# Row sums and first weight sums on VectorE, and a down stage with chunk-wise splits and four PSUM tiles, in a fused transformer block

## Chip, cores and metric

One core of one Trainium2 chip runs the whole kernel in one launch. The metric is the device time of that launch in microseconds (us), the median of several runs. Engines have short names: PE is TensorE (matrix products), DVE is VectorE, ACT is ScalarE, POOL is GpSimd, SP is SyncE, whose queue issues the DMAs. In the code they are T, V, A, G and S.

## What is computed

A block of a hybrid model on one sequence of 1024 tokens, 1024 features: adaptive norm, sparse attention and a gated linear attention side by side, output projection, and then the part that the change touches, a gated MLP with 2816 hidden features:

```python
x = x + g1[:, None, :] * mix
h2 = _modulate(_rms_norm(x, norm2_g[l]), sh2, sc2)
gate, up = jnp.split(h2 @ w_gate_up[l], 2, axis=-1)
x = x + g2[:, None, :] * ((jax.nn.silu(gate) * up) @ w_down[l])
return _rms_norm(x, final_g)
```

All inputs are fp32. Every large product is made of three passes: each operand is split in a high part, rounded to the type fp32r (a cast on ACT), and a low part, the rest (a subtraction on DVE or POOL), and high·high, high·low and low·high are added up in PSUM.

## The kernel before

**Mix and second norm (L1050 on).** A loop over eight token tiles t finishes the output projection of a tile (`mix_mm`, matmuls L1009 to L1011), adds it on DVE to the residual (L1012), norms it (`norm2`: square sum on ACT, scaling on POOL L1070), and stores the residual x1 to DRAM (x1_d). `norm2_T` transposes the normed tiles on PE (L1087), applies scale and shift on ACT (L1095) into the tiles `vv`, and splits them (`bsplit`, cast L1078, low part L1079).

**Gate and up (L1170 to L1222).** The two products are made by a scheme with seven products in place of eight, each of one block of weights or a sum of blocks with one block of activations or a sum of blocks. The sums of activations, t1 to t4, are the "row sums": made in `norm2_T` for the second half of the tokens, partly on DVE (L1102, L1105, L1109), partly on POOL (L1103, and the low halves of t3 and t4 in L1079). The sums of weights, s1 to s4, are made in `Pair.sum` on POOL (L1139, L1140, L1144, L1145). There are 11 pairs n of 256 hidden features; each has a gate and an up side, each with seven products k of 12 matmuls (L1170 high·high, L1171 high·low, L1172 low·high), 1848 matmuls in all. `PRODUCTS` names the operands of product k, `BANK` the PSUM bank; k = 0 and 4 use plain weights and the plain blocks 11 and 21, which are there first. The gate side takes four single PSUM banks (pool ps, 4 buffers), the up side two tiles of two banks (pool pw, 2 buffers); together that is all of PSUM. `wop` makes a weight operand: load (512 KB a half), sum if need be, cast on ACT (L1162), low part on DVE (L1163), seven products ahead. A written-out list `order` sets the sequence of products: in pair 0 product 0 and 4 of both sides, then 1, 2, 3, 5, 6 of gate and after that of up.

**Down (L1274 on).** The hidden features are 22 chunks f of 128, in groups of 2, 4, 4, 4, 4, 4. `down_ops` prepares all chunks of a group at once, while the group before is multiplied: load of 512 KB of w_down, scaling by g2 on POOL (L1292), cast on ACT (L1282) and low part on DVE (L1283); load of the hidden values from hid_d, cast and low part likewise. `down` runs over eight token tiles; for each the group's matmuls (L1319 to L1321, 6 for each chunk, 1056 in all) fill one pw tile, and DVE adds it to the residual tile x1 (L1324), which was read back before group 0 (L1278). In the last group the final norm follows (squares L1327, scaling L1304, store L1305).

Each engine works through its instructions in order. The buffers named here: g (33 tiles of 4 KB a partition), gs (4), raw (2), whi and wlo (4 each).

## Time and profile before

| what | us |
|---|---|
| median of 3 runs | 1489.37 (1487.27 to 1489.51) |
| profiled execution | 1487.22 |
| its span in the trace | 1485.5 |
| PE busy | 1346.8 (91%) |
| DVE busy | 895.8 (60%) |
| ACT busy | 563.5 (38%) |
| POOL busy | 452.9 (30%) |

The span is the time between the first and the last instruction that the profiler recorded; the execution's own time is a little longer. Busy times are shares of the whole span, through stages with different limits: what a stage waits for is read from the waits and the timeline of that stage. In a timeline an instruction stands with its start, its duration and, in brackets, how long its engine had been idle before it and who released it. Matmuls are pipelined, so their durations overlap, and the step from start to start is what one costs.

### The profile page before, as it was taken

The page shows a single profiled execution, that of the slowest core. Times are in us where ns is not written, and L with a number is a line of the kernel's source. Part 1 is how long each engine was busy: PE and PEld are TensorE (multiplying, and loading weights), DVE is VectorE, ACT ScalarE, POOL GpSimd, SP SyncE. Part 2 cuts the span into 40 slices and gives each one's busy share as a digit, 9 for nine tenths or more (in the row PEclk, how much of TensorE's full clock was granted, in tenths as well). Part 3 has the DMA queues.
Part 4 walks back from the last instruction along what each step waited for, and adds up shares of the span by engine and source line. Part 5 has one row for each costly group of instructions (what it writes and reads, how often), then busy time and mean ns, then how long its engine had stood idle before and what let it go on. Part 6 is the DMA issues. An engine that isn't in the chain of part 4 may idle for free.

```text
span 1485.5 us, 18355 instructions
## 1 busy us (share of the span) xinstructions
PE 1346.8 (91%) x6975; PEld 1124.7 (76%) x6975; DVE 895.8 (60%) x1544; ACT 563.5 (38%) x1009; POOL 452.9 (30%) x385
## 2 busy tenths in 40 slices
PE   5899856998899999999949999999999978999997
PEld 4777755797699888788837888888888856877786
DVE  4578999969538477663566445444545457345424
ACT  3466444666373333451654333333333223111201
POOL 3550531155000000140382444444444345113101
PEclk9999968998699999999978999999999998999999
DMA  9601001011013356360311222222223366113102
GB/s 267 184 15 43 15 1 29 29 29 44 15 30 101 113 151 204 104 237 1 114 42 30 85 85 85 86 86 85 85 79 106 129 233 205 57 57 113 43 3 111
DMA packets 91358, 131.11 MB, mean 88 GB/s; under 512 B 6179, under 2 KB 65666, under 8 KB 91270
## 3 DMA queue, kind: packets, MB, share of 16 engines
q1 hardware_dynamic: 91112, 129.88, 27.2%
q8 instruction: 55, 0.90, 0.2%
q14 instruction: 33, 0.27, 0.1%
q10 hardware_dynamic: 158, 0.06, 0.0%
HBM read 107.90 MB, written 22.03 MB: 87 GB/s over the span
## 4 chain that ended last, share of the span: by engine, by line
PE 60%; DVE 20%; DMA 6%; ACT 4%; POOL 4%; issue 3%; SPq 2%; DVEq 0%; ACTq 0%; POOLq 0%
PE pw L1170 5%; PE ps L1172 5%; PE ps L1170 5%; PE ps L1171 4%; PE pw L1172 4%; PE pw L1171 4%; PE pw L1319 4%; PE pw L1320 4%; PE pw L1321 4%; DVE junk_d L588 4%; DMA raw<-in_w_mod_dram 2%; DVE h L743 2%; PE pw L1009 2%; PE pw L1011 2%; PE pw L1010 2%
## 5 line engine op out<-in xcount | busy, mean ns | idle before, releaser
L617 ACT ACTIVATE junk_a<-g,Ya 128x1024 int8<-128x1024 f32 (+2 forms) x96 | 99.8, 1039 | 93.9 <-DVE Ya L624 92.9
L1324 DVE TENSOR_TENSOR g<-g,pw 128x1024 f32<-128x1024 f32 (+1 forms) x49 | 58.3, 1195 | 117.0 <-PE pw L1321 116.9
L246 PE MATMUL ps<-whi,g 128*128 128x256 f32 x384 | 114.4, 298 | 0.0
L247 PE MATMUL ps<-whi,g 128*128 128x256 f32 x384 | 113.1, 294 | 0.0
L248 PE MATMUL ps<-wlo,g 128*128 128x256 f32 x384 | 112.9, 294 | 0.0
L1292 POOL TENSOR_TENSOR raw<-raw,g 128x1024 f32<-128x1024 f32 x22 | 59.7, 2717 | 136.0 <-DMA raw<-in_w_down_dram 129.9
L1199 POOL TENSOR_TENSOR g<-g,h 128x512 f32<-128x512 f32 x33 | 52.3, 1585 | 141.7 <-DVE h L1213 66.9
L1170 PE MATMUL ps<-g,wlo 128*128 128x512 f32 x184 | 72.7, 395 | 17.4 <-ACT wlo L1162 17.4
L237 PE MATMUL ps<-g,whi 128*128 128x512 f32 x208 | 83.8, 403 | 0.0
L239 PE MATMUL ps<-g,wlo 128*128 128x512 f32 x208 | 82.6, 397 | 0.0
L238 PE MATMUL ps<-g,whi 128*128 128x512 f32 x208 | 82.1, 395 | 0.0
L1319 PE MATMUL pw<-g,g 128*128 128x512 f32 x192 | 76.4, 398 | 5.6 <-DVE g L1324 5.5
L246 PEld LDWEIGHTS ps<-whi,g 128*128 128x128 f32 x384 | 78.0, 203 | 1.6 <-issue 1.4
L1319 PE MATMUL pw<-whi,g 128*128 128x512 f32 x160 | 65.1, 407 | 14.5 <-DVE g L1324 14.0
L247 PEld LDWEIGHTS ps<-whi,g 128*128 128x128 f32 x384 | 77.9, 203 | 0.0
L248 PEld LDWEIGHTS ps<-wlo,g 128*128 128x128 f32 x384 | 77.8, 202 | 0.2 <-issue 0.2
L1320 PE MATMUL pw<-g,g 128*128 128x512 f32 x192 | 75.9, 395 | 0.0
L1321 PE MATMUL pw<-g,g 128*128 128x512 f32 x192 | 75.7, 394 | 0.0
L1172 PE MATMUL ps<-g,wlo 128*128 128x512 f32 x184 | 72.7, 395 | 3.2 <-DVE wlo L1163 3.2
L1170 PE MATMUL pw<-g,whi 128*128 128x512 f32 x184 | 73.9, 402 | 1.7 <-DVE h L1219 1.7
L954 POOL TENSOR_TENSOR raw<-raw,g 128x1024 f32<-128x1024 f32 x4 | 9.6, 2388 | 213.1 <-DMA raw<-in_w_out_dram 213.1
L1171 PE MATMUL ps<-g,wlo 128*128 128x512 f32 x184 | 72.5, 394 | 0.0
(378 smaller groups left out, 3863.1 us busy)
## 6 DMA issues: line engine op xcount, KB each, us to landing
raw<-in_w_gate_up_dram SPq DMA_DIRECT2D x40, 512.0 KB, 3.5
raw<-in_w_mod_dram SPq DMA_DIRECT2D x32, 512.0 KB, 3.6
raw<-in_w_in_dram SPq DMA_DIRECT2D x24, 512.0 KB, 3.7
hid_d<-g SPq DMA_DIRECT2D x22, 512.0 KB, 3.0
raw<-in_w_down_dram SPq DMA_DIRECT2D x22, 512.0 KB, 3.8
gs<-hid_d SPq DMA_DIRECT2D x22, 512.0 KB, 4.7
g<-in_x_dram SPq DMA_DIRECT2D x16, 512.0 KB, 6.2
g<-in_w_mod_dram SPq DMA_DIRECT2D x16, 512.0 KB, 8.6
```

Source lines behind the costliest of these rows:

```text
L237: T.matmul(pt, lhsT=wh, rhs=rh, start=(k == 0), stop=False)
L239: T.matmul(pt, lhsT=wl, rhs=rh, start=False, stop=(k == KC - 1))
L246: T.matmul(pt, lhsT=rh, rhs=wh, start=(k == 0), stop=False)
L247: T.matmul(pt, lhsT=rl, rhs=wh, start=False, stop=False)
L248: T.matmul(pt, lhsT=rh, rhs=wl, start=False, stop=(k == KC - 1))
L617: A.activation(junk_a[:, :W], score[t], AF.Sign, bias=Y[:, j:j + 1].bitcast(F32), accum_out=acc[:, j:j + 1])
L1170: T.matmul(pt, lhsT=w[:, 0, kk, :], rhs=rh, start=(not more and kk == 0), stop=False, skip_group_check=more)
L1171: T.matmul(pt, lhsT=w[:, 0, kk, :], rhs=rl, start=False, stop=False, skip_group_check=more)
L1172: T.matmul(pt, lhsT=w[:, 1, kk, :], rhs=rh, start=False, stop=(kk == 3), skip_group_check=more)
L1319: T.matmul(po[:, cc], lhsT=ah[:, r], rhs=wh[:, cc], start=(f == 0), stop=False)
L1320: T.matmul(po[:, cc], lhsT=al[:, r], rhs=wh[:, cc], start=False, stop=False)
L1321: T.matmul(po[:, cc], lhsT=ah[:, r], rhs=wl[:, cc], start=False, stop=(f == nf - 1))
```

## The change

It has three parts. (1) All row sums and their low parts are made on DVE, by `row_sums`: for the first half of the columns of blocks qq = 0 within the loop at t = 6, for the rest ("late", 128x512 and 128x1024 at a time) behind the loop, in the sequence t1, t3, 22, t2, t4. t2 takes the place of block 22 once that is split. (2) The first operands of pair 0 (products 0 and 4) come from loads of 128 columns (`first_ops`), its full weights are loaded behind the loop, its weight sums are made on DVE, its products 0 of gate and up run ahead of the last tiles' transposes and its products 4 between them, and products 1, 2, 3, 5, 6 then alternate between gate and up. PSUM banks are taken one by one. (3) In the down stage `down_op` prepares one chunk at every second token tile of the group before; odd token tiles take two ps banks and even ones a pw tile; ACT copies group 0 out of PSUM into new tiles `acc`, and x1 is read back and added in group 2.

The diff, with removed blocks shortened:

```diff
...
+X1_AT = 2
 
 C_Q, C_K, C_V, C_QI, C_KI, C_GQ, C_GK, C_GV, C_GO, C_GL = (
     0, 512, 1024, 1536, 2048, 2120, 2376, 2632, 3144, 3656)
@@ -1096,19 +1098,16 @@
                          bias=sh2[:, k:k + 1], scale=gg2[:, k:k + 1])
         if m == 0:
             bsplit(("11", "21")[kh], qq, v, cols, V)
...
+    def row_sums(names, qq, cols):
+
+        v11, v21, v12, v22 = (vv[key][:, :, cols] for key in ((0, 0, qq), (1, 0, qq), (0, 1, qq), (1, 1, qq)))
+        for name in names:
+            dst, a, b = {"t1": (v11, v12, v11), "t3": (v12, v22, v12), "22": (v22, None, None),
+                         "t2": (v22, v22, v11), "t4": (v21, v21, v22)}[name]
+            if a is not None:
+                V.tensor_tensor(dst, a, b, ALU.subtract)
+            bsplit(name, qq, dst, cols, V)
 
 
 
@@ -1124,7 +1123,12 @@
         def load(self, tag="raw"):
             self.raw = []
             for kh in range(2):
-                r = g([P, 4, 256]) if tag == "g" else g([P, 4, 256], tag="raw", bufs=NRAW)
+                if tag == "g":
+                    r = g([P, 4, 256])
+                elif tag == "ring":
+                    r = g([P, 4, 256], tag=("whi", "wlo")[kh], bufs=NW)
+                else:
+                    r = g([P, 4, 256], tag="raw", bufs=NRAW)
                 S.dma_start(r, w_gate_up[kh * 512:(kh + 1) * 512, self.c0:self.c0 + 256]
                             .rearrange("(k p) n -> p k n", p=P))
                 self.raw.append(r)
@@ -1133,16 +1137,17 @@
             return self.raw[j][:, :, i * P:(i + 1) * P]
 
         def sum(self, name):
+            E = V if self.n == 0 else G
             if name == "s1":
                 t = gs([P, 2, 4, P])
                 self.sums["s1"], self.sums["s2"] = t[:, 0], t[:, 1]
-                G.tensor_tensor(t[:, 0], self.a(1, 0), self.a(1, 1), ALU.add)
-                G.tensor_tensor(t[:, 1], t[:, 0], self.a(0, 0), ALU.subtract)
+                E.tensor_tensor(t[:, 0], self.a(1, 0), self.a(1, 1), ALU.add)
+                E.tensor_tensor(t[:, 1], t[:, 0], self.a(0, 0), ALU.subtract)
             elif name == "s3":
                 t = gs([P, 2, 4, P])
                 self.sums["s3"], self.sums["s4"] = t[:, 0], t[:, 1]
-                G.tensor_tensor(t[:, 0], self.a(0, 0), self.a(1, 0), ALU.subtract)
-                G.tensor_tensor(t[:, 1], self.a(0, 1), self.sums["s2"], ALU.subtract)
+                E.tensor_tensor(t[:, 0], self.a(0, 0), self.a(1, 0), ALU.subtract)
+                E.tensor_tensor(t[:, 1], self.a(0, 1), self.sums["s2"], ALU.subtract)
 
     uid_w = [0]
 
@@ -1181,13 +1186,15 @@
 
         def __init__(self, n, up, sg):
             self.pair, self.up, self.sg = Pair((DFF if up else 0) + n * 256, n), up, sg
-
-        def banks(self):
-            if self.up:
-                p, q = pw(), pw()
-                self.bank = [p[:, C0], p[:, C1], q[:, C0], q[:, C1]]
-            else:
-                self.bank = [ps() for _ in range(4)]
+            self.bank = [None] * 4
+
+        def banks(self, i):
+            if self.bank[i] is None and self.up:
+                p = pw()
+                self.bank[i // 2 * 2:i // 2 * 2 + 2] = [p[:, C0], p[:, C1]]
+            elif self.bank[i] is None:
+                self.bank[i] = ps()
+            return self.bank[i]
 
         def put(self, i, m, src):
             dst = self.sg[i][:, (C0, C1)[m]]
@@ -1199,10 +1206,8 @@
                 G.tensor_tensor(dst, dst, src, ALU.mult)
 
         def run(self, k, w):
-            if k == 0:
-                self.banks()
+            product(self.banks(BANK[k]), w, k)
             a, b, c, d = self.bank
-            product(self.bank[BANK[k]], w, k)
             if k == 0:
                 self.u2 = half()
                 A.copy(self.u2, a)
@@ -1227,8 +1232,7 @@
         two = [Side(n, False, None), Side(n, True, None)]
         sides.append(two)
         if n == 0:
-            order += [(s, k) for k in (0, 4) for s in two]
-            order += [(s, k) for s in two for k in (1, 2, 3, 5, 6)]
+            order += [(s, k) for k in (1, 2, 3, 5, 6) for s in two]
         elif n == NF - 1:
             order += [(s, k) for k in range(7) for s in two]
         else:
@@ -1240,22 +1244,50 @@
             s, k = todo.pop(0)
             ready.append(wop(s.pair, k, tag))
 
+    def first_ops(s):
+
+        raw = g([P, 8, P], tag="raw", bufs=NRAW)
+        S.dma_start(raw, w_gate_up[:, s.pair.c0:s.pair.c0 + P].rearrange("(k p) n -> p k n", p=P))
+        for j in range(2):
+            w = g([P, 2, 4, P], F32R)
+            A.copy(w[:, 0], raw[:, 4 * j:4 * j + 4, :])
+            V.tensor_tensor(w[:, 1], raw[:, 4 * j:4 * j + 4, :], w[:, 0].bitcast(F32), ALU.subtract)
+            first[s, 4 * j] = w
+
     xns = {}
+    first = {}
     nxt = att_pre(0)
     for t in range(NT):
         cur, nxt = nxt, att_pre(t + 1) if t + 1 < NT else None
         mix_mm(t, 0, *cur)
         xns[t] = norm2(t)
         if t == W0_AT:
...
+            for x in sides[0]:
+                first_ops(x)
         if t >= 2:
             for q in range(2):
                 norm2_T(t // 2 - 1, (2 * (t % 2) + q) if t < 6 else (q * 2 + t % 2))
-    for q in (0, 2, 1, 3):
+        if t == 6:
+            row_sums(("t1", "t3", "22", "t2", "t4"), 0, slice(0, 256))
+    sides[0][0].pair.load()
+    sides[0][1].pair.load("ring")
+    sg = [g([P, L]) for _ in range(2)]
+    for x in sides[0]:
+        x.sg = sg
+        x.run(0, first[x, 0])
+    for q in range(2):
         norm2_T(3, q)
+    late = ((0, slice(256, 512)), (1, slice(0, 512)))
+    for qq, cols in late:
+        row_sums(("t1",), qq, cols)
+    for n, x in enumerate(sides[0]):
+        x.run(4, first[x, 4])
+        norm2_T(3, 2 + n)
+    for name in ("t3", "22", "t2", "t4"):
+        for _ in range(2):
+            prepare()
+        for qq, cols in late:
+            row_sums((name,), qq, cols)
     for s, k in order:
         if k == 0 and not s.up:
             sg = [g([P, L]) for _ in range(2)]
@@ -1272,10 +1304,7 @@
 
 
     g2b = mod_bcast(1, 5 * D)
-    x1 = {}
-    for t in range(NT):
-        x1[t] = g([P, D])
-        S.dma_start(x1[t], x1_d[t * P:(t + 1) * P, :])
+    fin, acc = {}, {}
 
     def split_tile(raw, tags):
         hi, lo = (g([P, D], F32R) if tag == "g" else g([P, D], F32R, tag=tag, bufs=NW) for tag in tags)
@@ -1283,67 +1312,75 @@
         V.tensor_tensor(lo, raw, hi.bitcast(F32), ALU.subtract)
         return hi, lo
 
...
+    def down_op(n, f):
+
+        raw = g([P, D], tag="raw", bufs=NRAW)
+        S.dma_start(raw, w_down[f * P:(f + 1) * P, :])
+        G.tensor_tensor(raw, raw, g2b, ALU.mult)
+        rawh = gs([P, L])
+        S.dma_start(rawh, hid_d[f * P:(f + 1) * P, :])
+        hid = split_tile(rawh, ("g", "g"))
+        return hid, split_tile(raw, ("whi", "wlo") if n % 2 else ("g", "g"))
 
...
+    groups = [range(0, 2)] + [range(f, f + 4) for f in range(2, DFF // P, 4)]
+    NDG = len(groups)
+    cur, nxt = [down_op(0, f) for f in groups[0]], []
+    left = []
+    for n in range(NDG):
+        ending = n == NDG - 1
+        ahead = list(groups[n + 1]) if not ending else []
         for t in range(NT):
-            po = pw()
+            if t % 2 == 0 and ahead:
+                nxt.append(down_op(n + 1, ahead.pop(0)))
+            if n == X1_AT:
+                xr = gs([P, D])
+                S.dma_start(xr, x1_d[t * P:(t + 1) * P, :])
+            if t % 2:
+                po = [ps(), ps()]
+            else:
+                pq = pw()
+                po = [pq[:, C0], pq[:, C1]]
             r = slice(t * P, (t + 1) * P)
...
+            for m in range(2):
+                for f, ((ah, al), (wh, wl)) in enumerate(cur):
+                    cc = (C0, C1)[m]
+                    T.matmul(po[m], lhsT=ah[:, r], rhs=wh[:, cc], start=(f == 0), stop=False)
+                    T.matmul(po[m], lhsT=al[:, r], rhs=wh[:, cc], start=False, stop=False)
+                    T.matmul(po[m], lhsT=ah[:, r], rhs=wl[:, cc], start=False, stop=(f == len(cur) - 1))
+            if n == 0:
+                acc[t] = g([P, D])
+                for m, cc in enumerate((C0, C1)):
+                    A.copy(acc[t][:, cc], po[m])
+                continue
+            parts = [(C0, po[0]), (C1, po[1])] if t % 2 else [(slice(0, D), pq)]
+            ssq = small(2, tag="s2") if ending else None
+            for m, (cc, src) in enumerate(parts):
+                add = V.tensor_tensor(acc[t][:, cc], acc[t][:, cc], src, ALU.add)
+                if ending:
                     jk = gs([P, D], BF16)
-                    A.activation(jk[:, :w], x1[t][:, cc], AF.Square, accum_out=ssq[:, n:n + 1])
-            if last:
-                if w < D:
+                    A.activation(jk[:, cc], acc[t][:, cc], AF.Square, accum_out=ssq[:, m:m + 1])
+            if n == X1_AT:
+                V.tensor_tensor(acc[t], acc[t], xr, ALU.add)
+            if ending:
+                if len(parts) > 1:
                     V.tensor_tensor(ssq[:, 0:1], ssq[:, 0:1], ssq[:, 1:2], ALU.add)
                 left.append((t, rstd_of(ssq, D, 1)))
                 if len(left) > 1:
                     with tc.issue_after(add.ins):
                         finish_rows(*left.pop(0), D)
-        while left:
-            with tc.issue_after(add.ins):
-                finish_rows(*left.pop(0), 512 if len(left) == 0 else D)
-
-    groups = [range(0, 2)] + [range(f, f + 4) for f in range(2, DFF // P, 4)]
-    nxt = down_ops(0, groups[0])
-    for n in range(len(groups)):
-        cur, nxt = nxt, down_ops(n + 1, groups[n + 1]) if n + 1 < len(groups) else None
-        if nxt is None:
+        cur, nxt = nxt, []
+        if n == NDG - 2:
             fin["g"] = gs([P, D])
             S.dma_start(fin["g"], final_g[None, :].to_broadcast([P, D]))
-        down(*cur, nxt is None)
+    while left:
+        with tc.issue_after(add.ins):
+            finish_rows(*left.pop(0), 512 if len(left) == 0 else D)
 
 
 # ---- launch: one core; inputs and outputs as the reference has them ----
```

The order of PE where the mix ends and gate and up begins; ps_... and pw_... are PSUM tiles, L1087 (L1089 in the change) are transposes, L1170 to L1172 (L1175 to L1177) the product matmuls. Before:

```order
L1087 MATMUL ps_6745<-ident,gs_6618 128x128
L1170 MATMUL pw_6837<-g_6349,g_6420 128x512
L1171 MATMUL pw_6837<-g_6350,g_6420 128x512
L1172 MATMUL pw_6837<-g_6361,g_6420 128x512
L1170 MATMUL pw_6837<-g_6361,g_6420 128x512
L1087 MATMUL ps_6767<-ident,gs_6618 128x128
L1171 MATMUL pw_6837<-g_6362,g_6420 128x512
L1172 MATMUL pw_6837<-g_6361,g_6420 128x512
L1087 MATMUL ps_6738<-ident,gs_6694 128x128
```

Now:

```order
L1089 MATMUL ps_6700<-ident,gs_6552 128x128
L1175 MATMUL ps_6718<-g_6349,g_6411 128x512
L1176 MATMUL ps_6718<-g_6350,g_6411 128x512
L1177 MATMUL ps_6718<-g_6361,g_6411 128x512
L1175 MATMUL pw_6733<-g_6349,g_6419 128x512
L1177 MATMUL pw_6733<-g_6361,g_6419 128x512
L1089 MATMUL ps_6748<-ident,gs_6614 128x128
L1089 MATMUL ps_6755<-ident,gs_6689 128x128
L1175 MATMUL ps_6718<-g_6433,g_6414 128x512
L1177 MATMUL ps_6718<-g_6445,g_6414 128x512
L1089 MATMUL ps_6783<-ident,gs_6614 128x128
```

Before, the product 0 of one side (pw_6837) stood between transposes of the last two tiles; now both sides' products 0 (ps_6718, pw_6733) stand ahead of the last transposes, and product 4 (again ps_6718) behind eight of them.

The order of POOL in the same place, before, from the scaling of the last tile on (L1139 to L1145 weight sums, L1103 a row sum, L1079 the low part of one):

```order
L1070 TENSOR_SCALAR gs_6694<-g_6128,rs_6691 128x1024
L1139 TENSOR_TENSOR gs_6798<-raw_6409,raw_6411 128x512
L1103 TENSOR_TENSOR g_6702<-g_6710,g_6702 128x2x256
L1140 TENSOR_TENSOR gs_6798<-gs_6798,raw_6409 128x512
L1144 TENSOR_TENSOR gs_6804<-raw_6409 128x512
L1145 TENSOR_TENSOR gs_6804<-raw_6411,gs_6798 128x512
L1139 TENSOR_TENSOR gs_6853<-g_6413,g_6415 128x512
L1144 TENSOR_TENSOR gs_6872<-g_6413 128x512
L1103 TENSOR_TENSOR g_6626<-g_6634,g_6626 128x2x256
L1140 TENSOR_TENSOR gs_6853<-gs_6853,g_6413 128x512
```

The order of DVE now, from just behind the addition that ends the mix (L1109 row sums, L1081 low parts, L1144 and L1145 weight sums, L1168 low parts of weights):

```order
L1081 TENSOR_TENSOR g_6649<-g_6630,g_6648 128x2x256
L1109 TENSOR_TENSOR g_6430<-g_6430,g_6630 128x2x256
L1144 TENSOR_TENSOR gs_6810<-raw_6708,raw_6710 128x512
L1081 TENSOR_TENSOR g_6654<-g_6430,g_6653 128x2x256
L1145 TENSOR_TENSOR gs_6810<-gs_6810,raw_6708 128x512
L1144 TENSOR_TENSOR gs_6816<-whi_6712,wlo_6714 128x512
L1145 TENSOR_TENSOR gs_6816<-gs_6816,whi_6712 128x512
L1168 TENSOR_TENSOR wlo_6813<-gs_6810,wlo_6813 128x512
L1168 TENSOR_TENSOR whi_6819<-gs_6816,whi_6819 128x512
L1109 TENSOR_TENSOR g_6346<-g_6622,g_6346 128x2x256
L1109 TENSOR_TENSOR g_6358<-g_6697,g_6358 128x1024
```

The weight sums of pair 0 and all row sums moved from POOL's order into DVE's, where they stand in one queue with the low parts of the operands.

The order of DVE in the down stage, before, from the first additions of group 0 on (L1324 additions out of PSUM, L1283 low parts):

```order
L1324 TENSOR_TENSOR g_9707<-g_9707,pw_9801 128x1024
L1324 TENSOR_TENSOR g_9709<-g_9709,pw_9815 128x1024
L1283 TENSOR_TENSOR g_9753<-raw_9749,g_9752 128x1024
L1283 TENSOR_TENSOR g_9759<-gs_9756,g_9758 128x1024
L1283 TENSOR_TENSOR g_9766<-raw_9762,g_9765 128x1024
L1283 TENSOR_TENSOR g_9772<-gs_9769,g_9771 128x1024
L1324 TENSOR_TENSOR g_9711<-g_9711,pw_9829 128x1024
L1324 TENSOR_TENSOR g_9713<-g_9713,pw_9843 128x1024
L1283 TENSOR_TENSOR g_9779<-raw_9775,g_9778 128x1024
```

Now, around the first additions, which are those of group 1 (L1364 additions, L1312 low parts):

```order
L1312 TENSOR_TENSOR g_9909<-gs_9906,g_9908 128x1024
L1312 TENSOR_TENSOR g_9913<-raw_9903,g_9912 128x1024
L1312 TENSOR_TENSOR g_9976<-gs_9973,g_9975 128x1024
L1312 TENSOR_TENSOR g_9980<-raw_9970,g_9979 128x1024
L1312 TENSOR_TENSOR g_10043<-gs_10040,g_10042 128x1024
L1364 TENSOR_TENSOR g_9745<-g_9745,pw_9916 128x1024
L1364 TENSOR_TENSOR g_9762<-g_9762,ps_9942 128x512
L1312 TENSOR_TENSOR g_10047<-raw_10037,g_10046 128x1024
L1312 TENSOR_TENSOR g_10110<-gs_10107,g_10109 128x1024
L1364 TENSOR_TENSOR g_9762<-g_9762,ps_9943 128x512
L1312 TENSOR_TENSOR g_10114<-raw_10104,g_10113 128x1024
```

Group 0 has no additions on DVE any more; the low parts of group 1 follow one another, and those of the first chunks of group 2 stand ahead of group 1's first addition. The additions of odd token tiles come in halves from ps banks.

## Rows read from the trace of the kernel before

**Rows 1.** Windows: busy PE, PEld, DVE, ACT, POOL (instructions), granted clock, DMA share, GB/s.
```profile
750.00:800.00 50.00, 25.99 (x102) 20.05 (x101) 34.20 (x32) 25.69 (x47) 36.24 (x27) 0.73 0.10 32
825.00:1200.00 375.00, 375.00 (x1643) 306.58 (x1642) 182.19 (x241) 114.40 (x191) 157.23 (x104) 1.00 0.29 97
1205.50:1260.00 54.50, 41.89 (x160) 32.07 (x159) 42.84 (x29) 16.17 (x17) 25.84 (x11) 0.91 0.69 236
1260.00:1300.00 40.00, 40.00 (x178) 33.11 (x177) 14.32 (x12) 5.90 (x6) 6.73 (x3) 1.00 0.17 54
```
**Rows 2.** Waits of PE from 690 us on: total us, times, longest.
```profile
PE pw L1319 <- DVE g L1324: 19.4, 6, 6.1
PE ps L1170 <- ACT wlo L1162: 17.4, 1, 17.4
```
**Rows 3.** Timeline of PE: last mix matmul, transposes, a full-speed run of products.
```profile
748.89 0.40 PE L1011 MATMUL pw<-wlo,h 128*128 128x512 f32 x1
749.12 1.25 PE L1087 MATMUL ps<-ident,gs 128*128 128x128 f32 x10
...
825.13 0.39 PE L1170 MATMUL ps<-g,wlo 128*128 128x512 f32 x1
...
825.81 0.39 PE L1170 MATMUL ps<-g,wlo 128*128 128x512 f32 x1
```
**Rows 4.** Timeline of POOL: first weight sum of pair 0 and of pair 1.
```profile
757.31 1.70 POOL L1139 TENSOR_TENSOR gs<-raw,raw 128x512 f32<-128x512 f32 x1
...
792.81 1.29 POOL L1139 TENSOR_TENSOR gs<-raw,raw 128x512 f32<-128x512 f32 x1 [7.31 <-DMA raw<-in_w_gate_up_dram]
```
**Rows 5.** Timeline of DVE: end of the mix, a low part beside POOL, two without POOL.
```profile
752.79 1.21 DVE L1012 TENSOR_TENSOR g<-g,pw 128x1024 f32<-128x1024 f32 x1
...
766.22 1.75 DVE L1079 TENSOR_TENSOR g<-g,g 128x512 fp32r<-128x512 f32 x1
...
787.18 0.68 DVE L1163 TENSOR_TENSOR whi<-gs,whi 128x512 fp32r<-128x512 f32 x1
787.78 0.68 DVE L1163 TENSOR_TENSOR wlo<-gs,wlo 128x512 fp32r<-128x512 f32 x1
```
**Rows 6.** Timeline of ACT: the first cast of a weight sum.
```profile
779.29 0.61 ACT L1162 CAST wlo<-gs 128x512 fp32r<-128x512 f32 x1
```
**Rows 7.** Timeline of PE in the down stage: its first matmul, two waits, the last matmul.
```profile
1205.53 0.39 PE L1319 MATMUL pw<-whi,g 128*128 128x512 f32 x1
...
1225.30 0.80 PE L1319 MATMUL pw<-whi,g 128*128 128x512 f32 x1 [6.10 <-DVE g L1324]
...
1230.16 0.41 PE L1321 MATMUL pw<-wlo,g 128*128 128x512 f32 x1
...
1350.03 0.79 PE L1319 MATMUL pw<-g,g 128*128 128x512 f32 x1 [2.89 <-DVE g L1324]
...
1477.03 0.39 PE L1321 MATMUL pw<-g,g 128*128 128x512 f32 x1
```
**Rows 8.** Timeline of DVE in the down stage: splits ahead of additions, an addition in group 1.
```profile
1218.38 2.33 DVE L1283 TENSOR_TENSOR g<-raw,g 128x1024 fp32r<-128x1024 f32 x1 [3.36 <-ACT g L1282]
...
1222.90 1.21 DVE L1283 TENSOR_TENSOR g<-gs,g 128x1024 fp32r<-128x1024 f32 x1
1224.03 2.34 DVE L1324 TENSOR_TENSOR g<-g,pw 128x1024 f32<-128x1024 f32 x2
...
1267.79 1.22 DVE L1324 TENSOR_TENSOR g<-g,pw 128x1024 f32<-128x1024 f32 x1 [4.22 <-PE pw L1321]
```
**Rows 9.** Groups of the down stage by form (POOL, ACT), and a DMA issue.
```profile
L1292 POOL TENSOR_TENSOR raw<-raw,g 128x1024 f32<-128x1024 f32 x20 | 54.9, 2749 | 132.2 <-DMA raw<-in_w_down_dram 129.9 <-DVE g L1324 2.3
L1282 ACT CAST g<-gs 128x1024 fp32r<-128x1024 f32 x21 | 21.7, 1046 | 0.0
...
raw<-in_w_down_dram SPq DMA_DIRECT2D x22, 512.0 KB, 3.8
```
**Rows 10.** Timeline of DVE at the end: the last tile's two additions.
```profile
1477.46 1.28 DVE L1324 TENSOR_TENSOR g<-g,pw 128x512 f32<-128x512 f32 x2 [3.02 <-PE pw L1321]
```

49 lines of the change are left out of this document (2 added, 47 removed).

## The prediction

> **What bounds the kernel now.** I read the page first, then the windows of the second half of the span, then the waits of TensorE there, and last the timelines around the two places where TensorE stops. The windows [rows 1] show where there is anything to gain: in 825 to 1200 us TensorE is busy 375.00 of 375 us at granted clock 1.00, so for the ten later pairs of gate and up nothing on the other engines can matter. It is busy 25.99 of 50 us in 750:800 (granted clock 0.73) and 41.89 of 54.5 in 1205.5:1260. These are the stretches that the change edits. The waits [rows 2] name what ends last there: one wait of 17.4 us on the first operand made of a weight sum, and six waits of together 19.4 us on the DVE addition that empties a PSUM tile of the down stage.
>
> **Price of a product.** At full clock matmuls start (825.81 − 825.13) / 3 = 0.2267 us apart [rows 3], so a product of 12 takes 2.72 us; from 1225.30 to 1230.16 us eleven take 4.86 us, 0.44 each, which is the lower clock level (1.2 of 2.4 GHz), after a wait of 6.10 us [rows 7]. Such a spell therefore costs 4.86 − 2.49 = 2.4 us on top of its wait. The wait of 2.89 us at 1350.03 brought it too (that matmul's record is 0.79 long, like the 0.80 at 1225.30) [rows 7].
>
> **Start of gate and up, before.** Between the last matmul of the mix (748.89 us) and the first position at which both orders are the same again (825.13 us; 192 product matmuls and 24 transposes lie between) 76.2 us pass. The matmuls are worth 192 × 0.2267 = 43.5 and the transposes 24 × 0.125 = 3.0 (ten took 1.25) [rows 3]: 46.5 us. So 29.5 us are lost. POOL is why: from 757.31 it runs the weight sums L1139 to L1145 of both sides and the row sums L1103 and L1079 back to back, 1.70 us for 128x512 beside DVE, and the first cast of a weight sum is issued at 779.29, behind casts that wait for POOL [rows 4, 6].
>
> **The same stretch, after.** POOL loses the eight weight sums of pair 0 and the row sums; DVE gets them. A 128x512 subtraction on DVE takes 1.75 us beside a busy POOL and 0.68 alone, starting 0.60 apart [rows 5]; a 128x1024 one 1.21, the next starting 1.13 later [rows 8]. Between the addition that ends the mix and the operand of pair 1's first product DVE has 41 operations: 9 of 1024 elements and 32 of 512, 9 × 1.13 + 32 × 0.60 = 29.4 us, begun at about 753 (that addition began at 752.79 before [rows 5]) and waiting some 2 us in all for ACT and TensorE: 784.3 us if POOL stays quiet. POOL then has only the normalised rows of the last tile until pair 1's weights have landed (some 3.8 us after issue, as the loads of w_down, of the same size [rows 9]; their buffers come free near 777), so from 781 on its sums of 1.29 us [rows 4] meet the end of this queue. Four DVE operations that then cost 1.75 rather than 0.60 add 4.6 us: I take 788.9. The Trainium skill (SBUF — State Buffer, section "Who interferes with whom") says that a DVE instruction with two SBUF inputs and a GpSimd instruction that reads SBUF exclude each other for a whole instruction; the trace agrees in kind, and by that rule the four would cost 0.60 + 1.29 = 1.89 each, 0.6 us more in all.
> TensorE does not wait for that at first. After tile 6's transposes both products 0 start at 750.1, as the first did before, and take 24 × 0.2267 = 5.4 us to 755.6; their operands are loaded and split within the loop. Tile 7's normalised rows are there at about 754.8 (the mix addition ends near 751.5 to 753; square 1.2, rstd 0.8, scaling 1.2), so eight transposes, the two products 4 with four transposes behind each take TensorE without a wait to 762.6. By then row sum t1 is split; products 1 run to 768.5. Counted along the DVE queue, the low half for products 2 comes 0.7 us late (end 774.7) and t2 for products 3 about 1.5 us (end 781.7). Then the order has pair 1's first product, whose low half stands at the end of the DVE queue: a wait of 7.2 us to 788.9, then half clock (2.4 us). From there to the common position are 72 matmuls, 16.3 us: 788.9 + 16.3 + 2.4 = 807.6, a **gain of 17.5 us**. Bounds: 784.3 + 16.3 = 800.6 with no spell (gain 24.5), and four more contended operations, 812.2 (gain 12.9). What moved at no cost: the two loads of 128 columns replace loads of the same stage (DMA share 0.10 in 750:800 [rows 1]); if that cover were gone, product 0 would wait their 3.8 us. The loads of pair 0 now stand on SP behind the mix, and they land long before product 1.
>
> **Later pairs.** Same order of products and POOL sums as before; TensorE is full there. Nothing, between 0 and 0.3 us either way.
>
> **Down stage, before.** From 1205.53 to the start of the last matmul, 1477.03, plus one step of 0.23, 271.7 us pass [rows 7]. 1056 matmuls are worth 239.4. So 32.3 us are lost: 19.4 in the six waits [rows 2] and 12.9 in half clock, in the step after each wait and in waits under 0.7 us at the head of the stage. The timeline of DVE shows the cause [rows 8]: splits L1283 from 1218.38 on, the last at 1222.90, and only then the additions L1324 at 1224.03, while TensorE with two PSUM tiles has stood for 6.10 us when it goes on at 1225.30 [rows 7].
>
> **The same stretch, after.** Group 0 is copied out by ACT, so nothing stands in front of its eviction on DVE; ACT has 16 copies of 512 elements, about 0.61 each as its casts of that size [rows 6], and eight casts of 1.05 [rows 9], 18.2 us of the 21.8 that the group's 96 matmuls take. PSUM holds four tiles rather than two: TensorE may run 10.9 us ahead in group 0 and 21.8 later, more than the five splits that now stand ahead of group 1's first addition (5 × 1.13 = 5.7 us; one that met POOL took 2.33 [rows 8]). A chunk costs 3.8 us of load, 2.75 POOL, 1.05 ACT and 1.2 DVE [rows 8, 9]; with two raw buffers two chunks pass in about 8.8 us. Four need 17.6 of 21.8 us in group 0. Walked through: the raw buffers come free at about 1205, the first two chunks are there at 1209, scaled at 1214.2, split at 1216.4; the fourth takes over the second's buffer, 1216.4 + 3.8 + 2.75 + 1.05 + 1.2 = 1225.2, and 1.7 for ACT's copies and POOL's contention make 1226.9. TensorE starts group 1 at 1205.5 + 21.8 = 1227.3 and wants that chunk after nine matmuls, at 1229.4: a margin of 2.5 us. Later groups take 43.5 us each, margin over 7. The eight reads of x1 and the eight additions of 1.13 us in group 2 lie in DVE idle time of 4.2 us per tile [rows 8]. So I take all 32.3 us back. Bounds: 25 (one wait of 5 us with half clock stays) and 32.9 (also a wait of 0.6 just before the stage). **Gain 32.3.**
>
> **Tail.** The last tile's two halves are added together after the last matmul, 1.28 us [rows 10]; with two separate banks the first half goes earlier: 0.6 us (0 to 1).
>
> **Sum.** 17.5 + 32.3 + 0.6 = 50.4 us. The profiled execution took 1487.22 us (span 1485.5, so 1.7 lie around it): 1436.8. The median of the runs shown, 1489.37, lies 2.15 above it: **1439 us**. About 0.2% (3 us) is what a measurement of this kernel tells from no change.
>
> **Rivals.**
> 1. *DVE becomes the bound at the start.* Everything now goes through one queue in order. If the t2 and t4 sums also slip (late ACT casts), each of three products waits 2 to 3 us more: common position at 815, gain 10; sum 43, 1446 us, to 1451 with two more half-clock spells. For: the queue has 29.4 us of work in a stretch of 29. Against: POOL's contention is gone from most of it. Chance 0.15.
> 2. *The chunk chain is late at a change of group.* One wait of 6.1 us with half clock at group 1 (2.5 us of margin is small, and ACT's copies stand behind casts that wait for POOL): 8.5 us, 1447.5. Chance 0.10. At all five changes with 2.89 + 2.4 us [rows 7]: 26.5 us, 1465.5. Against: from group 1 on 43.5 us stand for 17.6 of chain. Chance 0.03.
> 3. *The depth does not help.* The order still puts splits ahead of additions; if they wait long enough the six waits stay, and only the start and the tail gain: 1471. Against: additions are then late by 6.1 us, and four tiles cover 10.9. Chance 0.03.
> 4. *Slower.* TensorE falls to half clock at the changes of PSUM tile. If the short gap at each new bank is enough, each of the 47 changes between the stage's 48 tiles costs a spell of 2.4 us: 112.8 − 50.4 = 62.4 more than now, 1552; it makes the kernel slower from 22 spells on (22 × 2.4 = 52.8). The Trainium skill tells of such a kernel (TensorE: Matmul & The Clock Gate, section "A second HAM failure mode: psum-queue depth-cycling"). Against it, by rows: 825 to 1200 changes bank with each product at clock 1.00, and so does 1260:1300 with tiles of 24 matmuls [rows 1]. Chance 0.02.
>
> **How the numbers follow.** The forecast gets 0.65: all best ends together (24.5 + 32.9 + 1.0) give 1431, and one bad end at a time 1443 (start) or 1446 (down). The single cases 1 and 2 have 0.25, rival 2 at all changes and rival 3 together 0.06, rival 4 0.02, and 0.02 is left for what I don't see. The range takes in the forecast, rival 1 and the single wait of rival 2, also both bad ends of the sum together with one more spell (1454), and leaves out the rest: 1430 to 1454. Faster by over 0.2%: forecast and rivals 1 to 3, 0.96. Slower: rival 4 and half of the unseen, 0.03. Same: the other half, 0.01.
>
> **What would show it.** Start: TensorE's wait on the low half of a weight sum, 17.4 us, is gone; products 0 and 4 of both sides run back to back from 750; one wait of 2.6 to 7.2 us before pair 1's first product; POOL has no L1144 before 780; the common position comes 13 to 24 us sooner. Down: TensorE's waits on the PSUM additions fall from six to none or one, granted clock 1.00 from 1200 on, and the stage takes 240 to 247 us. Wrong would be: a wait on the splits (L1312) at a change of group, ACT copies L1359 and on as releaser of PSUM, or a granted clock under 0.95 in the down stage.

## The result

The changed kernel takes 1440.56 us (median of 4 runs, 1440.18 to 1441.06), the kernel before 1488.32 in the same comparison; the ratio is 0.9684, 95% interval [0.9664, 0.9703]. Forecast were 1439, range 1430 to 1454. The profiled execution has a span of 1438.9 us, 46.6 less than before.

Runs of one kernel differ by up to some 20 us (those of the kernel before, in all comparisons here, lie between 1470.3 and 1491.9). In the traces most of that comes from a stretch near 350 to 430 us of the attention stage, which no kernel here alters: the mix's last matmul started at 738.3 us in one profiled execution and at 753.0 in another. So everything below is read by stretches of the profiled execution, counted from the start of the mix's last matmul. The common position is the first matmul from which both kernels have the same order again.

| us | before | change |
|---|---|---|
| last matmul of the mix | 748.89 | 751.44 |
| from there to the common position | 76.2 | 57.4 |
| from the mix's last matmul to the first down matmul | 456.6 | 439.9 |
| down stage, first to last matmul and one step | 271.7 | 239.8 |
| start of the last matmul to the end | 8.5 | 8.0 |

The stretches to the first down matmul, of the down stage and behind it gained 16.7 + 31.9 + 0.5 us; less the 2.55 by which the mix ended later in this execution, that makes the 46.6. The windows of the changed kernel (columns as in [rows 1]):

```profile
750.00:800.00 50.00, 41.90 (x186) 33.18 (x185) 45.95 (x58) 29.57 (x50) 12.87 (x9) 0.93 0.19 64
1200.00:1260.00 60.00, 60.00 (x266) 49.53 (x265) 39.70 (x29) 24.59 (x32) 22.31 (x9) 1.00 0.44 144
1260.00:1300.00 40.00, 40.00 (x178) 33.14 (x177) 30.99 (x25) 5.59 (x6) 10.67 (x4) 1.00 0.56 180
1191.30:1431.00 239.70, 239.67 (x1057) 197.93 (x1056) 132.12 (x117) 56.24 (x77) 59.71 (x35) 1.00 0.34 115
```

TensorE's busy time in 750:800 went from 25.99 to 41.90 us, POOL's from 36.24 to 12.87, and DVE's from 34.20 to 45.95: DVE is the fullest engine now. In the down stage (the last line) TensorE has no gap and granted clock 1.00 throughout; in 1205.5:1260 before, [rows 1], it was idle for 12.6 us. TensorE's waits from 745 us to the last matmul, where [rows 2] had 17.4 and six of together 19.4 us:

```profile
PE ps L1177 <- DVE wlo L1168: 6.2, 1, 6.2
PE ps L1175 <- DVE h L1217: 1.9, 1, 1.9
PE pw L1175 <- DVE h L1224: 1.5, 1, 1.5
PE ps L1175 <- ACT g L1080: 0.7, 1, 0.7
PE ps L1089 <- POOL gs L1072: 0.7, 1, 0.7
PE ps L1176 <- DVE g L1081: 0.4, 1, 0.4
```

No wait on an addition of the down stage (L1364) is left. The first two are the price of the start; the third, at the end of gate and up, was there before too (1.7 us). The timeline on PE (L1013 the last mix matmul, 808.88 the common position, 1191.35 the first down matmul):

```profile
751.44 0.40 PE L1013 MATMUL pw<-wlo,h 128*128 128x512 f32 x1
...
784.83 0.39 PE L1176 MATMUL ps<-g,wlo 128*128 128x512 f32 x1
791.45 0.79 PE L1177 MATMUL ps<-g,wlo 128*128 128x512 f32 x1 [6.23 <-DVE wlo L1168]
...
794.58 0.40 PE L1175 MATMUL ps<-g,wlo 128*128 128x512 f32 x1
...
808.88 0.39 PE L1175 MATMUL ps<-g,wlo 128*128 128x512 f32 x1
...
819.11 0.50 PE L1175 MATMUL ps<-g,whi 128*128 128x512 f32 x1 [1.91 <-DVE h L1217]
...
1191.35 0.39 PE L1353 MATMUL pw<-g,g 128*128 128x512 f32 x1
...
1430.91 0.39 PE L1355 MATMUL ps<-wlo,g 128*128 128x512 f32 x1
```

The 6.23 us are the wait before the third matmul of pair 1's first product. On DVE, in front of it, the low part that it needs is the row at 789.65 (L1168 from raw), and POOL's sums for pair 1 begin at 783.68:

```profile
783.48 0.68 DVE L1081 TENSOR_TENSOR g<-g,g 128x512 fp32r<-128x512 f32 x1
784.08 1.78 DVE L1168 TENSOR_TENSOR wlo<-gs,wlo 128x512 fp32r<-128x512 f32 x1
785.78 2.28 DVE L1081 TENSOR_TENSOR g<-g,g 128x1024 fp32r<-128x1024 f32 x1
787.98 1.74 DVE L1168 TENSOR_TENSOR whi<-gs,whi 128x512 fp32r<-128x512 f32 x1
789.65 1.75 DVE L1168 TENSOR_TENSOR wlo<-raw,wlo 128x512 fp32r<-128x512 f32 x1
791.32 0.68 DVE L1168 TENSOR_TENSOR whi<-gs,whi 128x512 fp32r<-128x512 f32 x1
```
```profile
783.68 1.62 POOL L1144 TENSOR_TENSOR gs<-raw,raw 128x512 f32<-128x512 f32 x1 [24.73 <-DVE g L1109]
```

Four operations that meet POOL: from 784.08 to the next start, at 791.32, they take 7.24 us, 4.3 more than their 0.60 and 1.13 alone.

### The profile page after: what moved, and what is told of

It reads as the page before. It is cut to its first block, busy times and chain, and to the rows that moved or that the text cites. A ratio compares the mean times of both kernels' runs of the same rounds, so it can differ in the third digit from the quotient of the medians.

```text
span 1438.9 us, 18354 instructions
## 1 busy us (share of the span) xinstructions
PE 1337.6 (93%) x6975; PEld 1121.2 (78%) x6975; DVE 899.8 (63%) x1577; ACT 571.7 (40%) x1026; POOL 423.7 (29%) x365
## 4 chain that ended last, share of the span: by engine, by line
PE 64%; DVE 19%; DMA 5%; issue 4%; ACT 3%; SPq 2%; POOL 2%; ACTq 0%; DVEq 0%; POOLq 0%
PE pw L1175 4%; PE pw L1176 4%; PE pw L1177 4%; PE ps L1177 4%; PE ps L1175 4%; PE ps L1176 4%; DVE junk_d L590 4%; PE pw L1353 3%; PE ps L1353 3%; PE pw L1355 3%; PE ps L1355 3%; PE pw L1354 3%; PE ps L1354 3%; DMA raw<-in_w_mod_dram 2%; DVE h L745 2%
## 5 line engine op out<-in xcount | busy, mean ns | idle before, releaser
L1319 POOL TENSOR_TENSOR raw<-raw,g 128x1024 f32<-128x1024 f32 x22 | 58.7, 2676 | 110.0 <-DMA raw<-in_w_down_dram 103.2
L241 PE MATMUL ps<-g,wlo 128*128 128x512 f32 x208 | 82.6, 397 | 0.0
L1177 PE MATMUL ps<-g,wlo 128*128 128x512 f32 x192 | 75.6, 394 | 6.3 <-DVE wlo L1168 6.2
L1175 PE MATMUL pw<-g,whi 128*128 128x512 f32 x192 | 76.9, 400 | 1.5 <-DVE h L1224 1.5
L1175 PE MATMUL ps<-g,wlo 128*128 128x512 f32 x192 | 75.4, 393 | 0.7 <-ACT g L1080 0.7
L1176 PE MATMUL ps<-g,wlo 128*128 128x512 f32 x192 | 75.3, 392 | 0.4 <-DVE g L1081 0.4
L1176 PE MATMUL pw<-g,whi 128*128 128x512 f32 x192 | 74.9, 390 | 0.0
L1177 PE MATMUL pw<-g,whi 128*128 128x512 f32 x192 | 74.8, 390 | 0.0
L590 DVE TENSOR_SCALAR_CACHE_REDUCE junk_d<-g,Zd 128x640 bf16<-128x640 f32 (+5 forms) x96 | 71.4, 744 | 1.8
L1168 DVE TENSOR_TENSOR whi<-gs,whi 128x512 fp32r<-128x512 f32 x44 | 37.8, 858 | 45.3 <-ACT whi L1167 44.7
L757 PE MATMUL pw<-h,gs 128*128 128x128 f32 x224 | 34.9, 316 | 30.5 <-DVE ma L622 16.4
```

The lines of the kernel that those rows point to most:

```text
L590: V.tensor_scalar(junk_d[:, :W], top[t] if 0 < i < 16 else score[t], Z[:, j:j + 1].bitcast(F32), -float(TOPK), ALU.is_ge, ALU.add, accum_o ...
L1175: T.matmul(pt, lhsT=w[:, 0, kk, :], rhs=rh, start=(not more and kk == 0), stop=False, skip_group_check=more)
L1176: T.matmul(pt, lhsT=w[:, 0, kk, :], rhs=rl, start=False, stop=False, skip_group_check=more)
L1177: T.matmul(pt, lhsT=w[:, 1, kk, :], rhs=rh, start=False, stop=(kk == 3), skip_group_check=more)
```

## The experiments

All kernels compute the whole result. The table has each profiled execution's stretches and the median of its runs (for the size of a part read the stretches: the medians carry the attention stage's spread).

| run | mix to first down matmul | down stage | median |
|---|---|---|---|
| before | 456.6 | 271.7 | 1488.3 |
| change | 439.9 | 239.8 | 1440.6 |
| start alone | 439.9 | 271.7 | 1473.6 |
| down alone | 456.5 | 240.2 | 1454.6 |
| row sums alone | 446.7 | 266.3 | 1480.6 |
| pair 0's sums on POOL | 443.8 | 239.7 | 1441.3 |
| depth alone (with the start) | 442.4 | 244.5 | 1439.9 |
| two tiles (with the start) | 442.6 | 248.0 | 1452.4 |
| x1 first | 439.3 | 245.5 | 1447.2 |
| pair 1's gate sums on DVE | 438.2 | 240.1 | 1438.7 |
| pair 1's sums on DVE, stores later | 432.2 | 240.4 | 1430.6 |
| stores later | 439.4 | 240.3 | 1432.5 |
| by side | 435.1 | 239.9 | 1435.1 |
| pair 1's sums, stores later and by side | 431.4 | 240.4 | 1430.6 |

**Start alone** and **down alone** cut the change in two. The first is the change with the down stage of the kernel before, its diff against the change; the second is the kernel before with the down stage of the change, its diff against the kernel before.

```diff
-    def down_op(n, f):
+    def down_ops(n, fs):
...
```


> The change's start (row sums, first operands and weight sums on DVE, alternating order) with the down stage of before. Theory of two separate gains: the start alone is worth 46.6 us of span less what the down stage gave back (31.9) and the tail (0.5), so 14 to 17 us: about 1472 us; PE's waits on L1324's counterpart stay, six or so, near 19 us in all, and the last down matmul comes 271 us after the first. Rival (the parts need each other: banks or buffers handed over differently at the end of gate and up): outside 1467 to 1477.

Measured: ratio 0.9922 [0.9896, 0.9949], 1473.6 us (the kernel before 1487.4 in the same comparison). TensorE waits on the additions seven times:

```profile
PE pw L1351 <- DVE g L1356: 20.1, 7, 6.3
```

```diff
-    def down_ops(n, fs):
+    def down_op(n, f):
...
```


> The down stage of the change behind the start of before. Theory of two separate gains: 32 to 33 us, about 1456; the stage takes 240 us from first to last matmul and PE does not wait on additions out of PSUM; the 17.4 us wait at the first weight sum stays. Rival: outside 1451 to 1461.

Measured: ratio 0.9792 [0.9728, 0.9855], 1454.6 us; the only wait left in the stage is 0.2 us. Both stretches come out within 0.4 us of the whole change's: the two gains are separate.

**Row sums alone** (against the kernel before).
```diff
-            G.tensor_tensor(v12, v22, v12, ALU.subtract)
+            V.tensor_tensor(v12, v22, v12, ALU.subtract)
...
-            bsplit("t3", qq, v12, cols, G)
+            bsplit("t3", qq, v12, cols, V)
...
-            bsplit("t4", qq, v21, cols, G)
+            bsplit("t4", qq, v21, cols, V)
```


> Before, with only the engine of the row sums t3 and t4 changed (five kinds of POOL operation go to DVE, in the places where they stand; order of products, loads and weight sums as before). Theory that POOL's queue is what PE waited for: POOL's eight weight sums then end some 8 operations x 1.3 us sooner or stand closer together, the 17.4 us wait shrinks to 8 to 12 us, total 1479 to 1484. Rival (the order and the late loads matter, not the engine): the wait moves to DVE's row sums, total within 3 us of 1488.

Measured: ratio 0.9956 [0.9927, 0.9984], 1480.6 us. TensorE's wait on the first weight sum:

```profile
775.06 0.80 PE L1170 MATMUL ps<-g,wlo 128*128 128x512 f32 x1 [11.19 <-ACT wlo L1162]
```

The 17.4 us became 11.2, and the stretch is 9.9 us shorter, of the 16.7 that the whole start gains: POOL's queue was a cause, and a change of engine in three lines is about half of the start's gain (by the medians, 6.8 of 13.8 us). The down stage, whose code is that of the kernel before, was 5.4 us shorter in this execution, with waits on additions of 17.0 rather than 19.4 us and 24 half-clock steps behind them rather than 37. So one execution gives the down stage's gain to some 5 us only.

**Pair 0's weight sums on POOL** (against the change, as all that follow unless said otherwise).
```diff
-            E = V if self.n == 0 else G
+            E = G
```


> The change with the weight sums of pair 0 back on POOL (eight operations of 128x512). If DVE and POOL shut each other out for whole operations, DVE's queue loses 8 x 0.60 = 4.8 us of own work and gains up to 8 x 1.1 = 8.8 of waiting: the wait before pair 1's first product grows from 6.2 to about 10 us, total 1443 to 1447. Rival (two engines share the work): the queue ends 4 to 5 us sooner, the wait shrinks to 2 us, total 1434 to 1437.

Measured: 1441.3 us, ratio 0.9713 [0.9645, 0.978]. Neither figure held. The low part for pair 1 ended 41.1 us after the start of the mix's last matmul (40.0 in the change), so DVE gained no time by losing 4.8 us of work, as the theory of exclusion said, but it lost 1.1 rather than 4. TensorE's waits:

```profile
PE ps L1177 <- DVE wlo L1168: 4.7, 1, 4.7
PE ps L1176 <- DVE g L1081: 3.2, 5, 1.4
```

The wait on that low part was 4.7 us, with five smaller ones on row sums ahead of it. The rest of the 3.9 us is half clock: 12 and 7 steps of 0.43 us after the two longest waits, against 6 in the change. By the medians (1441.3 and 1440.6) moving these sums to DVE can't be told from no change.

**Depth alone, two tiles, x1 first.** The first diff is against the run with the start alone, the other two against the change.
```diff
-            po = pw()
+            if t % 2:
+                po = [ps(), ps()]
+            else:
+                pq = pw()
+                po = [pq[:, C0], pq[:, C1]]
...
```


> The change's start, and of its down stage only the PSUM depth: odd token tiles in two ps banks, even ones in pw; splits of a whole group issued at once and x1 read at the start as before. Theory that the depth is what removes the waits: four tiles cover the four to six splits that stand ahead of an addition (up to 10 us), so PE's waits on additions go from 19.4 us to under 4, at least 22 of the 32 us come back: 1443 to 1450. Rival (the chunk-wise issue does it): the additions still come behind whole groups of splits, at least half of the loss stays, 1456 to 1472.

Measured: 1439.9 us (1430.6 to 1446.5), ratio 0.9682 [0.9621, 0.9743]; the stage 244.5 us. The median lies below the range expected, with an attention stage that was short in the profiled execution (the mix's last matmul at 739.7 us); the stage, on which the theory rests, is 4.7 us longer than the change's. TensorE's waits in it:

```profile
PE pw L1356 <- DVE g L1315: 1.9, 3, 1.0
PE pw L1355 <- DVE g L1360: 1.4, 1, 1.4
```

Additions (L1360) cost 1.4 us rather than 19.4; 27.2 of the 31.9 us come back, and no half-clock spell is left in the stage.

```diff
-            if t % 2:
-                po = [ps(), ps()]
-            else:
-                pq = pw()
-                po = [pq[:, C0], pq[:, C1]]
+            pq = pw()
+            po = [pq[:, C0], pq[:, C1]]
...
```


> The change with two PSUM tiles in the down stage (pw for all token tiles), splits chunk by chunk, group 0 copied out by ACT, x1 read in group 2. Theory that depth is needed: PE runs 10.9 us ahead from group 1 on and 5.4 in group 0, and five splits (5.7 us alone, up to 11 beside POOL) stand ahead of the first addition of a group: one wait of 2 to 6 us at most changes of group, 8 to 20 us in all, 1449 to 1461. Rival (chunks alone are enough): within 3 us of 1440.6.

Measured: 1452.4 us, ratio 0.9762 [0.9707, 0.9817]; the stage 248.0 us, 8.2 lost, as expected in size. The waits are others, though:

```profile
PE pw L1350 <- DVE h L1227: 2.7, 1, 2.7
PE pw L1350 <- ACT g L1356: 1.9, 2, 1.6
PE pw L1350 <- DVE g L1361: 0.9, 1, 0.9
```

TensorE hardly waits on additions (L1361) any more with two tiles either, when the splits come chunk by chunk, ACT copies group 0 out and x1 is added in group 2; what two tiles lack is room at the hand-over: gate and up's last evacuation (L1227, 2.7 us and a spell of 8 steps) and ACT's copies of group 0.

```diff
...
+    for t in range(NT):
+        acc[t] = g([P, D])
+        S.dma_start(acc[t], x1_d[t * P:(t + 1) * P, :])
...
-            if n == 0:
-                acc[t] = g([P, D])
-                for m, cc in enumerate((C0, C1)):
-                    A.copy(acc[t][:, cc], po[m])
-                continue
```


> The change with x1 read at the start of the down stage, as before, and added by DVE from group 0 on; no copies by ACT, no additions of 1.13 us in group 2. Theory that moving the eviction of group 0 to ACT and the reads to group 2 matters: eight loads of 512 KB go through SP ahead of the first chunks (about 3.3 us for six issues) and eight additions go between the splits of group 1: 3 to 9 us, 1443 to 1450. Rival (depth and chunks cover it): within 2 us of 1440.6.

Measured: 1447.2 us, ratio 0.9736 [0.9691, 0.978]; the stage is 5.7 us longer, with waits of together 4.3 us on low parts of groups 0 and 1:

```profile
PE pw L1357 <- DVE g L1315: 2.4, 2, 1.6
PE pw L1358 <- DVE wlo L1315: 1.1, 2, 0.6
PE pw L1358 <- DVE g L1315: 0.8, 1, 0.8
```

That the loads of x1 and the additions come in front of the chunks is argued from the order. So four tiles alone, or two tiles with everything else that the change does in the stage, remove nearly all waits on additions (chunk-wise splits with DVE's additions in group 0 and two tiles were not run), and the reads in group 2 together with ACT's copies of group 0 are worth 5.7 us at the head of the stage.

**The rest of the start.**
```diff
-            E = V if self.n == 0 else G
+            E = V if self.n == 0 or (self.n == 1 and self.c0 < DFF) else G
```


> The change with the four weight sums of pair 1's gate side on DVE too, where they stand behind the low part for pair 1's first product. If POOL's sums, issued from 783.7 us on, are what stretches the last four DVE operations to 1.74 to 2.28 us, those fall to 0.6 to 1.13: the wait of 6.2 us shrinks to about 1.6 and its half-clock spell (1.5 us) goes: 4 to 6 us less, 1434.5 to 1437. Rival (the wait only moves: DVE's own four sums and the low parts behind them make product 1 of pair 1 or the next side late): within 2 us of 1440.6.

Measured: 1438.7 us, ratio 0.9658 [0.9601, 0.9715]. The first wait fell to 1.9 us and had no spell, as said, but the next, on L1217, grew from 1.9 to 4.2 us with a spell of 8 steps:

```profile
PE ps L1175 <- DVE h L1217: 4.2, 1, 4.2
PE ps L1177 <- DVE wlo L1168: 1.9, 1, 1.9
```

Of the 4 to 6 us expected 1.7 are left by the stretch (1.9 by the median): the rival holds, the wait moved. What is late there is the up side of pair 1. Its second load is issued behind a store that waits for POOL, in the trace of the change:

```profile
804.37 0.34 SPq L1303 DMA_DIRECT2D hid_d<-g  x1
804.81 0.38 SPq L1132 DMA_DIRECT2D raw<-in_w_gate_up_dram  x1
```

Taking up the whole of pair 1, and the store:

```diff
...
-            E = V if self.n == 0 else G
+            E = V if self.n <= 1 else G
...
-        if k == 6 and s.up:
-            for i in range(2):
-                r0 = s.pair.n * 256 + i * P
+        if k == 6 and s.up and s.pair.n > 0 or k == 2 and s is sides[1][0]:
+            x = s if s.up else sides[0][1]
+            with nullcontext() if s.up else tc.issue_after(sides[1][1].pair.dma.ins):
...
```


> The change with the weight sums of pair 1 on DVE for both sides, and pair 0's stores of hidden values put behind pair 1's last load on SP's queue. Theory (after the run with pair 1's gate sums on DVE, the next wait, 4.2 us on L1217, comes from the up side: its second load is issued behind a store that waits for POOL, and its four sums run on POOL behind three multiplications): DVE is idle there for 5 us, so it makes the sums as soon as the load lands; the 4.2 us wait and its spell go. From the mix's last matmul to the first down matmul 432 to 435 us (438.2 in that run, 439.9 in the change). Rival (the wait moves on to pair 2, whose sums are still POOL's): 437 to 440.

Measured: 1430.6 us, ratio 0.9639 [0.9593, 0.9685]; the stretch 432.2, no wait on L1217, no half-clock spell. The store alone is that diff without the engine of the sums:

```diff
-        if k == 6 and s.up:
+        if k == 6 and s.up and s.pair.n > 0 or k == 2 and s is sides[1][0]:
...
```


> The change with only the order on SP's queue altered: pair 0's two stores behind pair 1's last load. The load was issued at 804.81 us, 1.6 us after its buffer came free, behind a store that waited 12.4 us for POOL. Theory that this store holds up the up side: the wait of 1.9 us on L1217 shrinks to 0.3, the stretch from the mix's last matmul to the first down matmul goes from 439.9 to 437.5 to 438.5. Rival (POOL's sums, not the load, are late): within 0.5 of 439.9, leaving half-clock spells aside.

Measured: 1432.5 us (1424.5 to 1442.5), ratio 0.9633 [0.9566, 0.97]. The wait of 1.9 us went entirely, but the wait of 6.2 us drew a spell of 13 steps rather than 6 in this execution, so the stretch shows 0.5 us. Without the seven more steps, 0.2 us each, it would be about 438.0, as the theory said.

```diff
-            order += [(s, k) for k in (1, 2, 3, 5, 6) for s in two]
+            order += [(s, k) for s in two for k in (1, 2, 3, 5, 6)]
```


> The change with pair 0's products 1, 2, 3, 5, 6 in the order gate first, then up, in the list (weights are prepared in that order too). Theory that alternating hides the row sums, which come every 5 to 6 us from DVE: each of gate's products 2, 3 and 5 would wait some 3 us for its row sum, and the stretch from the mix's last matmul to the first down matmul grows by 3 to 9 us over 439.9. Rival (DVE's queue is the bound anyway and the scheduler fills in the up side): within 2 us.

Measured: 1435.1 us, ratio 0.9668 [0.9622, 0.9714]; the stretch is 4.8 us shorter, not longer. No half-clock spell is left, and the waits are short:

```profile
PE pw L1175 <- DVE h L1224: 1.5, 1, 1.5
PE ps L1089 <- POOL gs L1072: 1.2, 1, 1.2
PE ps L1175 <- DVE h L1215: 1.2, 1, 1.2
```

The first of these is in the change too. Gate's raw tiles are read out sooner, so pair 1's load lands sooner and POOL's sums run within DVE's queue rather than at its end. That alternation costs time here is shown; that the earlier load is the whole reason is argued from this trace.

Both together, the diff of pair 1's sums and stores and this one:

```diff
-            E = V if self.n == 0 else G
+            E = V if self.n <= 1 else G
...
-            order += [(s, k) for k in (1, 2, 3, 5, 6) for s in two]
+            order += [(s, k) for s in two for k in (1, 2, 3, 5, 6)]
...
```


> The run with pair 1's sums on DVE and the stores put back (432.2 us from the mix's last matmul to the first down matmul), and in addition pair 0's products by side instead of alternating, which alone gave 435.1. Theory that both remove the same thing (POOL's sums for pair 1 meeting the end of DVE's queue, and the low part that stands there): no sum of the two gains, 431 to 434, the wait of 1.9 us on the low part goes and waits of under 1.3 us on row sums come instead. Rival (independent gains, 7.7 + 4.8): 427 to 429. Second rival (the small waits for row sums add up): 435 or more.

Measured: 1430.6 us (1430.3 to 1432.9), ratio 0.9625 [0.9603, 0.9646]; the stretch 431.4, as said for one cause behind both. It and the run with pair 1's sums and stores are about 10 us below the change by the medians, 8.5 and 7.7 by the stretch, each with runs of a narrow range; they don't differ from each other.

## Why the prediction held

- **Start.** The walk gave 58.7 us from the mix's last matmul to the common position (807.6 − 748.89); 57.4 were measured. The wait stood where it was forecast, before pair 1's first product, 6.23 us rather than 7.2, with a spell of 1.5 rather than 2.4 us (seven steps from 791.45 to 794.58, less seven at full clock). The low part was forecast 40.0 us after that matmul (788.9 − 748.89) and ended 40.0 after it (791.40 − 751.44). The kind of the queue was right (41 operations, some 2 us of waits, four operations beside POOL), but that the figures agree so closely is luck. The queue starts behind the addition below, at 754.10, 2.7 us after the mix's last matmul rather than the 4.1 of the forecast (753 − 748.89), and it lasted 37.3 rather than 35.9 us: the four operations cost 4.3 rather than 4.6 us extra, and earlier ones were late, one of them beside POOL's scaling of the last rows.

```profile
752.97 1.22 DVE L1014 TENSOR_TENSOR g<-g,pw 128x1024 f32<-128x1024 f32 x1
...
758.00 1.49 DVE L1145 TENSOR_TENSOR gs<-gs,whi 128x512 f32<-128x512 f32 x1
```

The Trainium skill (SBUF — State Buffer, section "Who interferes with whom") says that a DVE instruction with two SBUF inputs contends with a GpSimd instruction that reads SBUF, and the trace agrees: from start to start the 128x512 low parts beside POOL's sums took 1.67 to 1.70 us, against 0.60 alone. The estimate of 1.89 us that the prediction worked out by that rule was above that. Not run by themselves were the loads of 128 columns and the early products 0 and 4; alternating, which the change has, cost time (the run by side). In the prediction's sums, the 29.5 us lost before should be 29.7 (76.2 − 46.5); nothing rests on it.
- **Later pairs** was the step that failed: "nothing, between 0 and 0.3 us" was 1.9 of wait and 0.2 of restart at 819.11. The wait before it had been placed on DVE's queue and not followed on to what was late next, the up side of pair 1 with its load behind a store on SP; with that store put later the 1.9 us went.
- **Down.** 32.3 forecast, 31.9 measured. The reason given, that four tiles cover the splits ahead of an addition, is sufficient by itself (depth alone), but not the only cure: two tiles with the rest of the stage's change hardly wait on additions either. The margin of 2.5 us at group 1 did not hold. The fourth chunk of that group was forecast 21.4 us after the stage's first matmul (1226.9 − 1205.5); its last low part ended 24.3 us after it (1215.63 − 1191.35), and the matmul that reads it started 0.1 us later:

```profile
1213.45 2.17 DVE L1312 TENSOR_TENSOR g<-gs,g 128x1024 fp32r<-128x1024 f32 x1 [1.18 <-ACT g L1311]
```
```profile
1215.72 0.47 PE L1354 MATMUL pw<-whi,g 128*128 128x512 f32 x1
```

So it was luck that the chain of splits cost nothing there. In the runs with down alone, stores later, pair 1's sums and stores, and all three together TensorE waits 0.2 to 0.4 us on that low part.
- **Tail.** 0.6 forecast, 0.5 measured. Executions with the old tail end 8.5 to 9.0 us after the start of the last matmul, those with the new one and four tiles 7.9 to 8.4, so single executions show it barely.
- **Rivals.** Number 1 did not occur: DVE's queue ends last before pair 1's first product, but that was in the forecast, and the waits on row sums that the rival put at 2 to 3 us for each of three products were 0.7 and 0.4 us. Number 2 did not occur either, by 0.1 us, nor did number 3. Number 4 fell: with PSUM tiles changed 47 times the granted clock is 1.00 in 1191:1431, the upper level. The Trainium skill's case of a changing PSUM queue (TensorE: Matmul & The Clock Gate, section "A second HAM failure mode: psum-queue depth-cycling") is therefore not this stage's.
- **Sum.** The profiled execution was forecast at 1436.8 us and took 1440.6. The 3.8 us are 2.55 for the later mix, 2.1 for the missed wait and 0.5 at the down stage and the tail, less 1.3 at the start. That the forecast of the median came within 1.6 us is partly luck: the 2.15 us put on for the median were not there (it lies 0.04 below the profiled execution) and made up for most of the later mix. The 3 us by which the prediction would tell a change from none are too few for runs that differ by up to 20.

## What to carry to other kernels

When one engine's queue holds up TensorE, move its work and then read what the receiving queue ends with: here the last four operations met the other engine's next job. Moving that too, and putting off the store that held up the next load, was worth another 7.7 us of the stretch; moving half of it alone only moved the wait. More PSUM tiles alone took most of the waits on additions away, and so did a finer issue of the work ahead of them, with an earlier copy out of PSUM, on two tiles; try one cure alone before paying for both. After a wait is gone, look one consumer further on, DMA queues included. And where a wait that was feared did not come, read how much room was left: here 0.1 us.
